# Tracing an attention's results one product later, behind that product's weights

## The chip, the cores and the metric

The kernel runs on one core of a Trainium2 chip. The metric is device microseconds from start to end of one execution; three runs of the kernel before gave a median of 849.12 us (848.67 to 849.75). TensorE (PE in the profile, its weight loads PEld) multiplies, VectorE (DVE) and ScalarE (ACT) compute elementwise, GpSimd (POOL) makes masks and starts some DMAs, SyncE (SP) starts the other DMAs. Each engine works through its own queue in order.

## The reference

One decoder layer: `x + W_out[conv, FoX, memory](RMSNorm(x))`, then an RMSNorm, for 512 tokens of 2048 features, all in float32.

```python
proj = rmsnorm(x, norm_g) @ w_in            # cut into the inputs of the three groups
u = silu(layernorm(causal_depthwise_conv(cv_a * sigmoid(cv_b), 31 taps)))
y_conv = (u @ w_conv_pw) * silu(cv_gate)
# FoX, 8 heads of 128: logit[t,s] = q.k * scale + c[t] - c[s], causal, c = cumsum(log_sigmoid(f))
y_fox = softmax(logit) @ v * silu(fox_gate)
# memory, 4 heads of 128: cross-attention into 256 memory tokens
y_mem = softmax(q.mk * scale) @ mv * silu(mem_gate)
out = rmsnorm(x + concat(y_conv, y_fox, y_mem) @ w_out, final_g)
```

## The kernel before

Every float32 operand is split into a high part (float32r, a copy on ScalarE, line 93) and a low part (the rest, a subtraction on VectorE, line 94). `split` makes both, and three matmuls (hh, hl, lh) stand for one. A piece of weights, 128x1024, is loaded by SP into one of six buffers `raw` and split into one of three buffers `wb` by `operand`, which remembers the low part's instruction in `lows`.

The projections of the layer are made two column blocks of 128 at a time in `pair`, from about 120 to 675 us: seven products of half the depth on sums of inputs and sums of weights (line 512) stand for eight. A product is 24 matmuls of 256 columns. In the order of `pair` they multiply `a11`, `s1`, `s2`, `a12`, `s4`, `s3` and `a22`; in the names of the trace `s1`, `s2` and `s3` are s0h, s1h and s2h (low parts s0l, s1l, s2l), the others hh and hl.

Beside each product, `beside` puts other work. One step of `bg`, mostly one of the 30 taps of the depthwise convolution (line 384, `acc` on VectorE), is queued on VectorE behind the product's split by `tc.issue_after(low)`: an edge of order for the instructions of that engine, not a wait. Then one piece of `slots` is traced, with its TensorE instructions behind the product's last matmul. A piece of an attention holds some matmuls into a buffer `at` (three of them, in PSUM) and what ScalarE and VectorE make of these at once. For a FoX head (counted from 0) the pieces are: scores and softmax of the query blocks 0 and 1 (`probs`: `mm3` into `at`, then line 899 adds the bias and takes the row's extreme on VectorE, line 903 is the exponential on ScalarE, lines 904 and 905 divide by the sum); the same for blocks 2 and 3; the gate and values (`gate_values`); transposes of the probabilities (`attend`, split into `pth` and `ptl`); the product with the values. The memory heads go the same way (`mem_probs`, `mem_attend`).

The order of instructions on an engine is not the order of tracing alone: a scheduler sorts what is traced by a timeline of its own, within the edges.

The convolution's layer norm (`norm`, `over_channels`) and its projection (`project_conv`, weights in `csh` and `csl`) come before head 7, and the output product (lines 1048 to 1142) last.

Of the kernel before, what the change touches and what calls it, by code (L numbers as in the profile page):

```python
# [14 lines left out]
ALU = mybir.AluOpType  # L15
AX = mybir.AxisListType

P = 128
# [29 lines left out]
def hybrid_layer_kernel(  # L48
# [18 lines left out]
    nc = tc.nc  # L67
    x, mem, out = x[0], mem[0], out[0]
# [11 lines left out]
    def nm(s):  # L80
        uid[0] += 1
        return f"{s}_{uid[0]}"
# [28 lines left out]

    bg, slots = deque(), deque()
    lows = [None]

    def background(n):
        for _ in range(min(n, len(bg))):
            bg.popleft()()

    def raw_tile(n, c):
        return wp.tile([P, n, c], F32, tag="raw", name=nm("raw"), bufs=6)
# [390 lines left out]

    def beside(low, mm):
        with tc.issue_after(low):
            background(1)
        if slots:
            with tc.issue_after(mm):
                slots.popleft()()
# [72 lines left out]
    def mem_probs(h, q, pr, i2):  # L592
        qh, ql = q
        sp = at((P, 2, M))
        for j in range(2):
            sl = slice((2 * i2 + j) * P, (2 * i2 + j + 1) * P)
            mm3(sp[:, j, :], (qh[:, sl], ql[:, sl]), (mk[0][:, h, :], mk[1][:, h, :]), True, True)
        ng = ma.tile([P, 2], F32, tag="ng", name=nm("ng"), bufs=4)
        nc.vector.tensor_reduce(ng, sp, AX.X, ALU.max, negate=True)
        nc.vector.tensor_scalar(ng, ng, SC, None, ALU.mult)  # L600
        pp = ma.tile([P, 2, M], F32, tag="pp", name=nm("pp"), bufs=2)
        sm = ma.tile([P, 2], F32, tag="sm", name=nm("sm"), bufs=4)
        for j in range(2):
            nc.scalar.activation(
                pp[:, j, :], sp[:, j, :], AF.Exp,
                bias=ng[:, j : j + 1], scale=SC, accum_out=sm[:, j : j + 1],
            )
        nc.vector.reciprocal(sm, sm)
        for j in range(2):
            nc.scalar.mul(pp[:, j, :], pp[:, j, :], sm[:, j : j + 1])  # L610
        pr.append(pp)

    def mem_attend(h, pr, gate):

        pts, ov = {}, []

        def transposes(mt):
            tp = at()
            for i in range(NT):
                nc.tensor.transpose(  # L620
                    tp[:, i * P : (i + 1) * P], pr[i // 2][:, i % 2, mt * P : (mt + 1) * P], ident
                )
            pts[mt] = tuple(ma.tile([P, S], F32R, tag=t, name=nm(t)) for t in ("th", "tl"))
            split(*pts[mt], tp)

        def values(mt):
            if mt == 0:
                ov.append(at())
            hs = slice(h * P, (h + 1) * P)
            mm3(ov[0], (mv[0][:, mt, hs], mv[1][:, mt, hs]), pts[mt], mt == 0, mt == MT - 1)  # L630

        def end():
            values(1)
            nc.vector.tensor_tensor(gate[0], ov[0], gate[0], ALU.mult)
            nc.gpsimd.dma_start(out=yd[12 + h], in_=gate[0])

        return [lambda: transposes(0), lambda: (values(0), transposes(1)), end]

# [2 lines left out]
    def after_mem(h):  # L641
        def f(xs, col):
            q = mem_query(xs)
            pr, gate = [], []
            pieces = mem_attend(*mpending.pop()) if mpending else [lambda: None]
            end = pieces.pop()
            pieces.append(
                lambda: (end(), gate.append(mem_gate(col)), mem_probs(h, q, pr, 0))
            )
            pieces.append(lambda: mem_probs(h, q, pr, 1))  # L650
            mpending.append((h, pr, gate))
            if h < NM - 1:
                (log_sigmoid, running_sum, forget_columns)[h]()
            else:
                pieces.extend(mem_attend(*mpending.pop()))
                after = pieces.pop()

                def close():
                    after()
                    mapool.close()  # L660
                    fgpool.close()
                    mpool.close()
                    open_fox()

                pieces.append(close)
            slots.extend(pieces)

        return f
# [109 lines left out]
    pieces = w_pieces()  # L778
# [80 lines left out]
    def gate_values(xs, col):  # L859
        fx = fox["pool"]  # L860
        gate = fx.tile([P, S], F32, tag="fgate", name=nm("fgate"), bufs=2)

        for x_, g in zip(xs, halves(gate)):
            nc.scalar.activation(g, x_, AF.Tanh, scale=0.5)
            nc.vector.scalar_tensor_tensor(g, g, 1.0, x_, ALU.add, ALU.mult)
        vp = at()
        for j in range(NT):
            sl = slice(j * P, (j + 1) * P)
            nc.tensor.transpose(vp[:, sl], col[:, sl], ident)
        v = tuple(fx.tile([P, NT, P], F32R, tag=t, name=nm(t)) for t in ("vh", "vl"))  # L870
        split(*v, vp.rearrange("p (j d) -> p j d", d=P))
        return gate, v

    def biases(h):
# [16 lines left out]
    def probs(q, k, i, b):  # L891
        fx = fox["pool"]
        n = (i + 1) * P
        sl = slice(i * P, n)
        w = max(n, M)
        sp = at((P, w))
        mm3(sp, (q[0][:, sl], q[1][:, sl]), (k[0][:, :w], k[1][:, :w]), True, True)
        ng = fx.tile([P, 1], F32, tag="ng", name=nm("ng"), bufs=4)
        nc.vector.tensor_tensor_reduce(
            b, sp[:, :n], b, 1.0, -MASKED, ALU.add, ALU.min, accum_out=ng  # L900
        )
        sm = fx.tile([P, 1], F32, tag="sm", name=nm("sm"), bufs=4)
        nc.scalar.activation(b, b, AF.Exp, bias=ng, scale=-1.0, accum_out=sm)  # L903
        nc.vector.reciprocal(sm, sm)
        nc.scalar.mul(b, b, sm)

    def attend(h, gv, pr):

        pth, ptl = fox["h"], fox["l"]

        def transposes(j):
            n = S - j * P
            tp = at((P, n))
            for i in range(j, NT):
                nc.tensor.transpose(
                    tp[:, (i - j) * P : (i - j + 1) * P], pr[i][:, j * P : (j + 1) * P], ident
                )
            w = max(n, M)
            split(pth[j][:, w - n :], ptl[j][:, w - n :], tp)

        def values():
            gate, (vh, vl) = gv
            ov = at()
            for j in range(NT):
                w = max(S - j * P, M)
                mm3(
                    ov[:, S - w :], (vh[:, j, :], vl[:, j, :]), (pth[j], ptl[j]),
                    j == 0, j == NT - 1,
                )
            if h < NH - 1:  # L930
                nc.vector.scalar_tensor_tensor(gate, ov, 0.5, gate, ALU.mult, ALU.mult)
                nc.gpsimd.dma_start(out=yd[4 + h], in_=gate)
            else:
                nc.vector.scalar_tensor_tensor(last["y"], ov, 0.5, gate, ALU.mult, ALU.mult)

        return [lambda: (transposes(0), transposes(1)), lambda: (transposes(2), transposes(3)), values]
# [12 lines left out]
    def after_gv(h):  # L949
        def f(xs, col):  # L950
            gv = []
            slots.append(lambda: gv.extend(gate_values(xs, col)))
            slots.extend(attend(h, gv, pr.pop(h)))
            if h == NH - 2:

                def norm():
                    fpool.close()
                    with tc.high_priority():
                        open_norm()
                        centre()  # L960
                        normalise()

                slots.append(norm)

        return f

# [19 lines left out]
    for fa, fb, then in work + [(None, None, None)]:  # L986
        if fa is not None:
            steps = pair(fa, fb)
            next(steps)
        else:  # L990
            for _ in range(2):
                load_piece()
            plain_ys()
            for _ in range(3):
                load_piece()
            heads = [load_y(4 + i // 2 + i % 2 * 4, i) for i in range(7)]
            last["y"] = y_room(7)
            for j in range(3):
                head_ys(j, *heads[2 * j : 2 * j + 2])
        if before:  # L1000
            before[1](*next(before[0]))
        if fa is None:
            while slots:
                slots.popleft()()
        else:
            next(steps)
            before = (steps, then)
            if fa == F_Q + (NH - 1) * P:
                project_conv()
                lnpool.close()  # L1010
                open_fox()
# [197 lines left out]
```

## Time and profile before

| | us |
|---|---|
| median of three runs | 849.12 |
| the profiled execution, its time | 849.81 |
| the profiled execution, its span | 848.0 |
| PE busy | 824.6 |
| DVE busy | 717.3 |
| ACT busy | 472.6 |

The span is the time from the first to the last instruction in the trace. Busy time of TensorE is modelled from pipelined matmuls, so the time that it loses is read better from the starts of matmuls that follow each other.

### The profile page before, as it was taken

How to read it: one execution, taken by the hardware profiler on the slowest of the kernel's cores; microseconds unless marked ns; L12 is line 12 of the kernel's file. 1: busy time of each engine (PE TensorE's matmuls, PEld its weight loads, DVE VectorE, ACT ScalarE, POOL GpSimd, SP SyncE). 2: the span in 40 equal slices, each digit the busy share in tenths (PEclk: the TensorE clock that was granted, in tenths of full speed). 3: DMA queues.
4: the chain of work that ended last, by engine and by line, in shares of the span. 5: the costliest groups of instructions: out<-in, count | busy, mean ns of one | idle time of the engine just before them, and what ended most of it. 6: DMA issues, size and time to landing. Idle time of an engine off the chain costs nothing. (4 is left out here: it accounts for less than half of the span.)

```text
span 848.0 us, 15403 instructions
## 1 busy us (share of the span) xinstructions
PE 824.6 (97%) x6212; PEld 785.7 (93%) x6212; DVE 717.3 (85%) x1047; ACT 472.6 (56%) x778; POOL 59.2 (7%) x86
## 2 busy tenths in 40 slices
PE   7999999999999999999999999999979999999996
PEld 6898889999999999999999999999979988998995
DVE  4589999999889998899988999896986976976964
ACT  4775457456775564554656455555564933442423
POOL 1012000000011000011110020200001000000001
PEclk8999999999999999999999999999989999999999
DMA  8983213434434342533434343445344627361515
GB/s 308 336 229 78 77 26 102 125 100 113 124 101 109 101 113 76 146 100 96 106 92 128 100 109 100 124 112 163 100 124 151 210 82 266 100 216 35 154 44 198
DMA packets 144262, 109.76 MB, mean 129 GB/s; under 512 B 4060, under 2 KB 127032, under 8 KB 143552
## 3 DMA queue, kind: packets, MB, share of 16 engines
q1 hardware_dynamic: 142272, 103.57, 42.5%
q0 software_dynamic: 1920, 5.23, 1.8%
q8 instruction: 48, 0.79, 0.4%
q14 instruction: 22, 0.18, 0.1%
HBM read 99.55 MB, written 9.22 MB: 128 GB/s over the span
## 5 line engine op out<-in xcount | busy, mean ns | idle before, releaser
L94 DVE TENSOR_TENSOR wb<-raw,wb 128x1024 fp32r<-128x1024 f32 x232 | 282.9, 1222 | 59.5 <-ACT wb L93 59.1
L93 ACT CAST wb<-raw 128x1024 fp32r<-128x1024 f32 x232 | 241.3, 1050 | 161.4 <-PE pj L550 49.7
L550 PE MATMUL pj<-hh,wb 128*128 128x256 f32 x1536 | 286.0, 281 | 0.5 <-ACT wb L93 0.4
L550 PEld LDWEIGHTS pj<-hh,wb 128*128 128x128 f32 x1536 | 240.7, 189 | 1.7 <-ACT wb L93 0.9
L550 PE MATMUL pj<-hl,wb 128*128 128x256 f32 x768 | 214.6, 279 | 0.0
L550 PEld LDWEIGHTS pj<-hl,wb 128*128 128x128 f32 x768 | 145.0, 189 | 0.8
L512 DVE TENSOR_TENSOR raw<-raw,raw 128x1024 f32<-128x1024 f32 x112 | 136.2, 1216 | 0.4
L384 DVE SCALAR_TENSOR_TENSOR acc<-up,cwt,acc 128x512 f32<-128x512 f32 x120 | 89.2, 743 | 0.0
L1110 PE MATMUL pj<-wb,rh 128*128 128x256 f32 x672 | 79.9, 279 | 0.7 <-DVE sst L1164 0.4
L1110 PEld LDWEIGHTS pj<-wb,rh 128*128 128x128 f32 x672 | 79.3, 188 | 1.4 <-DVE res L1036 1.1
L550 PE MATMUL pj<-s1h,wb 128*128 128x256 f32 x384 | 74.1, 284 | 3.8 <-DVE wb L94 3.8
L550 PE MATMUL pj<-s2h,wb 128*128 128x256 f32 x384 | 73.8, 280 | 0.0
L550 PE MATMUL pj<-s0h,wb 128*128 128x256 f32 x384 | 71.0, 278 | 0.0
L550 PEld LDWEIGHTS pj<-s1h,wb 128*128 128x128 f32 x384 | 60.1, 188 | 4.7 <-DVE wb L94 4.6
L550 PEld LDWEIGHTS pj<-s2h,wb 128*128 128x128 f32 x384 | 60.8, 188 | 0.1
L550 PEld LDWEIGHTS pj<-s0h,wb 128*128 128x128 f32 x384 | 60.2, 188 | 0.0
L550 PE MATMUL pj<-s2l,wb 128*128 128x256 f32 x192 | 53.6, 279 | 0.0
L550 PE MATMUL pj<-s0l,wb 128*128 128x256 f32 x192 | 53.5, 279 | 0.0
L550 PE MATMUL pj<-s1l,wb 128*128 128x256 f32 x192 | 53.4, 278 | 0.0
L884 POOL TENSOR_SCALAR_AFFINE_SELECT b<-b 128x128 f32<-128x128 f32 x32 | 29.8, 938 | 226.5 <-ACT b L883 226.4
L550 PEld LDWEIGHTS pj<-s2l,wb 128*128 128x128 f32 x192 | 36.1, 188 | 0.1
L550 PEld LDWEIGHTS pj<-s1l,wb 128*128 128x128 f32 x192 | 36.1, 188 | 0.0
(300 smaller groups left out, 1358.9 us busy)
## 6 DMA issues: line engine op xcount, KB each, us to landing
raw<-in_w_in_dram SPq DMA_DIRECT2D x104, 512.0 KB, 4.2
raw<-in_w_out_dram SPq DMA_DIRECT2D x32, 512.0 KB, 4.7
raw<-in_w_mem_kv_dram SPq DMA_DIRECT2D x12, 512.0 KB, 7.5
xr<-in_x_dram SPq DMA_DIRECT2D x4, 1024.0 KB, 7.9
res<-in_x_dram SPq DMA_DIRECT2D x8, 512.0 KB, 6.9
out_dram<-res SPq DMA_DIRECT2D x16, 256.0 KB, 2.9
rs<-yd SPq DMA_DIRECT2D x15, 256.0 KB, 4.4
mr<-in_mem_dram SPq DMA_DIRECT2D x8, 256.0 KB, 8.0
```

The lines of the kernel that those rows point to most:

```text
L93: ins = nc.scalar.copy(hi, src)
L94: low = nc.vector.tensor_tensor(lo, src, hi.bitcast(F32), ALU.subtract)
L384: return lambda: nc.vector.scalar_tensor_tensor(acc, up[:, j : j + S], cwt[:, c, j : j + 1], acc, ALU.mult, ALU.add)
L512: nc.vector.tensor_tensor(o, p, q, ALU.subtract)
L550: mm = nc.tensor.matmul(o, p[:, k, :], q, start=start and k == 0 and i == 0, stop=k == HK - 1 and i == 2, skip_group_check=True,)
L884: nc.gpsimd.affine_select(out=b[:, sl], in_=b[:, sl], pattern=[[-1, P]], compare_op=ALU.is_ge, fill=-MASKED, base=0, channel_multiplier=1,)
L1110: nc.tensor.matmul(o[:, m, :], p, q[:, k, :], start=start and k + m + i == 0, stop=k == HK - 1 and i == 2, skip_group_check=True,)
```

## The change

A new queue `after` takes what ScalarE and VectorE make of an attention's matmuls. It is emptied (`results`) in `beside` of the next product, inside `issue_after(low)`, so behind that product's weight split on VectorE, before the tap and before the next piece. `mem_probs` and `probs` hand over their softmax this way, the transposes and the values their splits, the value products their gating. Before a pair's results are handed on (`before[1]`) and in the last round the queue is emptied as well.

```diff
+    bg, slots, after = deque(), deque(), deque()
...
+    def results():
+        while after:
+            after.popleft()()
...
     def beside(low, mm):
         with tc.issue_after(low):
+            results()
             background(1)
         if slots:
             with tc.issue_after(mm):
...
             mm3(sp[:, j, :], (qh[:, sl], ql[:, sl]), (mk[0][:, h, :], mk[1][:, h, :]), True, True)
+        after.append(lambda: mem_softmax(sp, pr))
+
+    def mem_softmax(sp, pr):
...
-            split(*pts[mt], tp)
+            after.append(lambda: split(*pts[mt], tp))
...
-            nc.vector.tensor_tensor(gate[0], ov[0], gate[0], ALU.mult)
-            nc.gpsimd.dma_start(out=yd[12 + h], in_=gate[0])
+            after.append(gated)
...
-        split(*v, vp.rearrange("p (j d) -> p j d", d=P))
+        after.append(lambda: split(*v, vp.rearrange("p (j d) -> p j d", d=P)))
...
         mm3(sp, (q[0][:, sl], q[1][:, sl]), (k[0][:, :w], k[1][:, :w]), True, True)
+        after.append(lambda: softmax(sp, n, b))
+
+    def softmax(sp, n, b):
+        fx = fox["pool"]
         ng = fx.tile([P, 1], F32, tag="ng", name=nm("ng"), bufs=4)
...
-            split(pth[j][:, w - n :], ptl[j][:, w - n :], tp)
+            after.append(lambda: split(pth[j][:, w - n :], ptl[j][:, w - n :], tp))
...
+            after.append(lambda: gated(gate, ov))
...
-                slots.append(norm)
+                slots.append(lambda: after.append(norm))
...
         if before:
-            before[1](*next(before[0]))
+            columns = next(before[0])
+            results()
+            before[1](*columns)
         if fa is None:
             while slots:
+                results()
                 slots.popleft()()
+            results()
```

The scheduler's result differs from before in few places: on VectorE in the FoX heads 1, 2, 4 and 6, where 28 rows stand differently in all, and in one row of ScalarE. The rows of TensorE, SP and POOL are the same in kind and order. In the rows below, `ISA` with `b` and `ng` is line 899 (line 913 after), the read of a score tile `at`; `wb` is a piece of weights; `acc` is a tap (line 384, after 389).

VectorE in head 1, before, from the low part of the queries `fq` on (`wb_3378` is the third product's):

```order
L512 TENSOR_TENSOR raw_3226<-raw_3230,raw_3226 128x1024
L97 SCALAR_TENSOR_TENSOR fq_3294<-pj_2966,fq_3293 128x256
L899 ISA b_3305,ng_3359<-at_3355,b_3305 128x128
L899 ISA ng_3359 128x1
L94 TENSOR_TENSOR wb_3378<-raw_3226,wb_3378 128x1024
L384 SCALAR_TENSOR_TENSOR acc_2829<-up_2828,cwt,acc_2829 128x512
L899 ISA b_3310,ng_3369<-at_3365,b_3310 128x256
L899 ISA ng_3369 128x1
L94 TENSOR_TENSOR wb_3428<-raw_3232,wb_3428 128x1024
L384 SCALAR_TENSOR_TENSOR acc_2829<-up_2828,cwt,acc_2829 128x512
L94 TENSOR_TENSOR wb_3456<-raw_3230,wb_3456 128x1024
```

The first score read stands ahead of the third product's split. VectorE at the same place after (`wb_3366` is the third product's):

```order
L517 TENSOR_TENSOR raw_3226<-raw_3230,raw_3226 128x1024
L97 SCALAR_TENSOR_TENSOR fq_3294<-pj_2966,fq_3293 128x256
L94 TENSOR_TENSOR wb_3366<-raw_3226,wb_3366 128x1024
L913 ISA b_3305,ng_3393<-at_3355,b_3305 128x128
L913 ISA ng_3393 128x1
L389 SCALAR_TENSOR_TENSOR acc_2829<-up_2828,cwt,acc_2829 128x512
L913 ISA b_3310,ng_3399<-at_3359,b_3310 128x256
L913 ISA ng_3399 128x1
L94 TENSOR_TENSOR wb_3416<-raw_3232,wb_3416 128x1024
L94 TENSOR_TENSOR wb_3456<-raw_3230,wb_3456 128x1024
L389 SCALAR_TENSOR_TENSOR acc_2829<-up_2828,cwt,acc_2829 128x512
```

The split of the third product has moved ahead of the first score read, and the second tap behind the fifth product's split; the third tap comes only after the rows shown. Heads 2, 4 and 6 change here in the same way; heads 0, 3, 5 and 7 have the split ahead of the score read in both kernels.

TensorE in head 1, before, the scores of query blocks 2 and 3, with the engine whose event a row waits for:

```order
L104 MATMUL at_3406<-fk_3295,fq_3293 128x384 [waits PE_49]
L105 MATMUL at_3406<-fk_3296,fq_3293 128x384
L106 MATMUL at_3406<-fk_3295,fq_3294 128x384
L104 MATMUL at_3416<-fk_3295,fq_3293 128x512 [waits PE_49]
L105 MATMUL at_3416<-fk_3296,fq_3293 128x512
L106 MATMUL at_3416<-fk_3295,fq_3294 128x512
```

The same rows after:

```order
L104 MATMUL at_3406<-fk_3295,fq_3293 128x384 [waits PE_49]
L105 MATMUL at_3406<-fk_3296,fq_3293 128x384
L106 MATMUL at_3406<-fk_3295,fq_3294 128x384
L104 MATMUL at_3410<-fk_3295,fq_3293 128x512 [waits DVE_49]
L105 MATMUL at_3410<-fk_3296,fq_3293 128x512
L106 MATMUL at_3410<-fk_3295,fq_3294 128x512
```

The instructions stand as they did; the first matmul of the 512-column tile, the fourth score tile of the head, now waits for an event of VectorE where it waited for one of TensorE. This, in the same four heads, is the only wait of TensorE that differs.

## Rows read from the trace of the kernel before

**Rows 1.** The page, part 1: busy us (share of the span) and instructions by engine.
```profile
PE 824.6 (97%) x6212; PEld 785.7 (93%) x6212; DVE 717.3 (85%) x1047; ACT 472.6 (56%) x778; POOL 59.2 (7%) x86
```

**Rows 2.** Waits: engine and line, for whom; us in total, times, longest us.
```profile
DVE wb L94 <- ACT wb L93: 62.9, 69, 4.4
...
PE pj L104 <- ACT csh L93: 4.5, 1, 4.5
...
PE pj L550 <- DVE wb L94: 3.8, 4, 0.9
```

**Rows 3.** Stretches: us; PE, PEld, DVE, ACT, POOL busy (count); PEclk; DMA share; GB/s.
```profile
285.00:330.00 45.00, 44.06 (x371) 43.59 (x371) 42.68 (x63) 25.48 (x46) 2.82 (x5) 1.00 0.39 106
...
375.00:440.00 65.00, 65.00 (x550) 64.60 (x549) 60.48 (x88) 37.30 (x67) 11.62 (x10) 1.00 0.42 114
```

**Rows 4.** Timeline of PE, first place: start, us, engine, line, op, tiles, count [idle before].
```profile
284.95 0.28 PE L550 MATMUL pj<-s1h,wb 128*128 128x256 f32 x1
...
285.30 0.28 PE L550 MATMUL pj<-hl,wb 128*128 128x256 f32 x1
286.52 0.51 PE L550 MATMUL pj<-s1h,wb 128*128 128x256 f32 x2 [0.94 <-DVE wb L94]
286.86 0.28 PE L550 MATMUL pj<-s1l,wb 128*128 128x256 f32 x1
```

**Rows 5.** Timeline of PE, the second to fourth place.
```profile
330.91 0.28 PE L550 MATMUL pj<-hl,wb 128*128 128x256 f32 x1
332.13 0.50 PE L550 MATMUL pj<-s1h,wb 128*128 128x256 f32 x2 [0.94 <-DVE wb L94]
...
441.50 0.51 PE L550 MATMUL pj<-s1h,wb 128*128 128x256 f32 x2 [0.94 <-DVE wb L94]
...
550.88 0.51 PE L550 MATMUL pj<-s1h,wb 128*128 128x256 f32 x2 [0.94 <-DVE wb L94]
```

**Rows 6.** Timeline of DVE, first place.
```profile
285.03 0.29 DVE L899 CUSTOM_DVE_ANT_0 b<-at,b 128x128 f32<-128x128 f32 x1 [2.03 <-PE at L106]
285.24 1.22 DVE L94 TENSOR_TENSOR wb<-raw,wb 128x1024 fp32r<-128x1024 f32 x1
```

**Rows 7.** Timeline of ACT, the casts at the first three places.
```profile
282.75 2.00 ACT L93 CAST wb<-raw 128x1024 fp32r<-128x1024 f32 x2 [0.71 <-DVE raw L512]
...
284.91 1.05 ACT L93 CAST wb<-raw 128x1024 fp32r<-128x1024 f32 x1
...
328.24 2.00 ACT L93 CAST wb<-raw 128x1024 fp32r<-128x1024 f32 x2 [0.60 <-DVE raw L512]
...
436.92 1.99 ACT L93 CAST wb<-raw 128x1024 fp32r<-128x1024 f32 x2
```

**Rows 8.** Timelines of ACT, DVE and PE in head 3.
```profile
392.78 1.99 ACT L93 CAST wb<-raw 128x1024 fp32r<-128x1024 f32 x2
...
393.86 1.23 DVE L94 TENSOR_TENSOR wb<-raw,wb 128x1024 fp32r<-128x1024 f32 x1 [0.52 <-ACT wb L93]
...
396.04 0.39 PE L550 MATMUL pj<-s1h,wb 128*128 128x256 f32 x2
```

**Rows 9.** Timelines of DVE and PE near the first place.
```profile
313.42 1.31 DVE L94 TENSOR_TENSOR wb<-raw,wb 128x1024 fp32r<-128x1024 f32 x1
...
299.98 0.74 DVE L384 SCALAR_TENSOR_TENSOR acc<-up,cwt,acc 128x512 f32<-128x512 f32 x1
300.64 0.41 DVE L509 TENSOR_TENSOR col<-pj,p 128x256 f32<-128x256 f32 x1
...
301.52 0.28 PE L550 MATMUL pj<-hh,wb 128*128 128x256 f32 x1
...
289.72 0.39 PE L104 MATMUL at<-fk,fq 128*128 128x512 f32 x1
```

**Rows 10.** Timelines of DVE and PE around the convolution's norm.
```profile
619.17 0.69 DVE L717 TENSOR_SCALAR spare<-at 128x512 f32<-128x512 f32 x1 [0.55 <-PE at L686]
...
630.56 0.79 PE L104 MATMUL pj<-csh,wb 128*128 128x512 f32 x1 [4.48 <-ACT csh L93]
```

More of the change, by code (lines that the diff above doesn't have):

```diff
@@ L109, in queued @@
         tc.keep_in_program_order(nc.sync.dma_start(out=dst, in_=src))
-    bg, slots = deque(), deque()
+    bg, slots, after = deque(), deque(), deque()
     lows = [None]
@@ L630, in values, with gated @@
             mm3(ov[0], (mv[0][:, mt, hs], mv[1][:, mt, hs]), pts[mt], mt == 0, mt == MT - 1)
+        def gated():
+            nc.vector.tensor_tensor(gate[0], ov[0], gate[0], ALU.mult)
+            nc.gpsimd.dma_start(out=yd[12 + h], in_=gate[0])
         def end():
             values(1)
-            nc.vector.tensor_tensor(gate[0], ov[0], gate[0], ALU.mult)
-            nc.gpsimd.dma_start(out=yd[12 + h], in_=gate[0])
+            after.append(gated)
         return [lambda: transposes(0), lambda: (values(0), transposes(1)), end]
@@ L647, in f @@
             pieces.append(
-                lambda: (end(), gate.append(mem_gate(col)), mem_probs(h, q, pr, 0))
+                lambda: (end(), after.append(lambda: gate.append(mem_gate(col))), mem_probs(h, q, pr, 0))
             )
@@ L655, in f @@
                 pieces.extend(mem_attend(*mpending.pop()))
-                after = pieces.pop()
                 def close():
-                    after()
                     mapool.close()
@@ L663, in close @@
                     open_fox()
-                pieces.append(close)
+                pieces.append(lambda end=pieces.pop(): (end(), after.append(close)))
             slots.extend(pieces)
@@ L929, in values, with gated @@
                 )
+            after.append(lambda: gated(gate, ov))
+        def gated(gate, ov):
             if h < NH - 1:
```

## The prediction

> **What bounds the kernel now.** I read the page first: TensorE is busy 97% of the span [rows 1], so a microsecond counts only where TensorE loses it. Then TensorE's own waits: the longest is one of 4.5 us before the convolution's projection, the next, on VectorE's weight split, comes four times at 0.9 us [rows 2]. The table of stretches says how they lie: from 285 to 330 us TensorE is 0.94 us short of full, and from 375 to 440 it is full to the hundredth [rows 3]. So the four are single events, not a spread-out loss.
>
> The timeline of the first [rows 4]: matmuls of 256 columns start every 0.117 us (284.95 to 285.30 is three of them), and the next would have started at 285.42; it starts at 286.52. So 1.10 us are lost. Of the three that start from there to 286.86 the two intervals take 0.34 instead of 0.23 us, so starting up again costs another 0.11. The profile's 0.94 of idle time is less, since it counts from the modelled end of the last matmul. The other three places, at 332.13, 441.50 and 550.88, read alike [rows 5]: at the second the starts are 1.22 us apart again (330.91 to 332.13), and each has the same 0.94 of idle time.
>
> What TensorE waits for there is the low part of the third product's weights (its stationary operand is a piece of wb, the moving one is s2, which the trace calls s1h). VectorE at the first place [rows 6]: it is done with all else at 283.00, sits idle 2.03 us until TensorE has made the first score tile (L106), reads it (L899, 0.29 us) and only then makes the low part of wb, from 285.24, 1.22 us long. ScalarE had long finished the high part that this needs [rows 7]: two casts begin at 282.75 and take 2.00 together, one alone takes 1.05, so the first ends at 283.80. The weights were ready to be split 1.44 us before they were, behind an instruction that waited for TensorE. The four places have this in common, and they are the four heads in which the orders of the two kernels differ; the other four have the split in front of the score read already.
>
> **The change part by part.** No instruction is added or removed; TensorE's, SP's and POOL's rows stand in the same order. *Split ahead of the score read, four heads.* After the cast's end at 283.80 the split runs to about 285.05 (the row's 1.22, and 0.03 from cast to start, as the control below shows), and TensorE can go 0.06 later (286.46 to 286.52 in rows 4 and 6): 285.11. It is wanted at 285.42, or, if the weights are loaded one matmul's step ahead, at 285.30. That leaves 0.2 us. At the second place the cast begins at 328.24, so TensorE can go at 330.60, and wants to at 330.91: 0.3 us. At the third the cast begins at 436.92 [rows 7], so TensorE can go at 439.28 and wants to at 440.28 (1.22 before 441.50, where the first place has its 285.30): 1.0 us. The fourth is like the third. So all four waits go: 4 x (1.10 + 0.11) = 4.84 us.
>
> That this order runs without a wait the kernel itself shows in head 3 [rows 8]: VectorE waits 0.52 us for the cast that began at 392.78, starts the split at 393.86 (cast 1.05, then 0.03), and TensorE begins the matmul that needs it, at 396.04, with no idle time ahead of it.
>
> *What stands behind the split.* The score read waits for TensorE until 285.03 anyway; the split ends at 285.05, so the read loses 0.02 us, and ScalarE's exponential of this tile has to wait for a cast that ends only at 285.96 (284.91 and 1.05, rows 7). Behind the read everything on VectorE comes 1.2 us sooner, as TensorE does: the slack of later weights stays as it is. The bound from the other side is a split that runs as long as the longest row I saw, 1.31 instead of 1.22 [rows 9]: 0.09 of the 0.2 us.
>
> *Taps.* One or two of the 0.74 us convolution taps (L384) move behind later splits of the same head. From the first moved one on, the splits of that head stand 0.66 us sooner (a tap's step to the next start) or as before. The tightest later point is the column sum at 300.64, ending at 301.05, which the last product wants before 301.52 [rows 9]: in front of it there is now one tap fewer. Where the tap comes back, behind it, VectorE is as far as TensorE again. I take 0; the bounds are 0.66 us won and 0.66 us lost per head, 2.6 in all, if a split behind a tap had no room.
>
> *The fourth score tile.* There are three buffers for score tiles, so the 512-column scores reuse the buffer of the first, and TensorE now waits there for VectorE's read of it (before, an older TensorE event covered it). That matmul begins at 289.72 [rows 9], 1.2 sooner after the change, so 288.5; the read is done by 285.4. Cost 0, with 3 us of room.
>
> *ScalarE.* In one head a multiplication (L905) goes ahead of a cast that in that place waits for TensorE. ScalarE is busy 25.48 of 45 us [rows 3]. Cost 0.
>
> *Is the gain kept to the end?* The one big wait behind the four is 4.5 us at 630.56 for the convolution's norm [rows 2, 10]. If that chain ran on a time of its own, TensorE would only wait there longer. But it contains matmuls: VectorE's step at 619.17 was waiting for TensorE's sum (L686), so it comes forward with TensorE. Nothing later waits on a clock of its own; the loads are issued as buffers come free.
>
> The sum, against the profiled execution's 849.81: 849.81 - 4.84 = 844.97. The median shown is 849.12, 0.69 under that execution, so the prediction is 844.3.
>
> **The rivals.**
> 1. *The two tight places keep their wait.* For it: 0.2 and 0.3 us of room is what a slower cast or split could eat, and in the stretch from 285 to 330 VectorE is busy 42.68 of 45 us. Against it: VectorE's lead there grows by as much as TensorE's, and head 3 passes. If the first two waits stayed whole, 849.12 - 2 x 1.20 = 846.7.
> 2. *The gaps stay:* the ring of three score buffers, or of three wb, is what TensorE waits for, and VectorE only passes it on. For it: the four gaps are equal to a hundredth [rows 4, 5]. Against it: the cast into this wb was written by 283.80, so its buffer was there, and VectorE sat idle, waiting for a matmul [rows 6, 7]. 849.1. The Trainium skill (Perfetto Trace Analysis, section Optimization Strategy) has this as a rule: the same gap repeating on the engine that should be saturated can mean too little SBUF or PSUM for the next tile to be allocated. By that rule a new order on VectorE would win nothing; the trace disagrees, in the rows just named.
> 3. *The waits go but the end doesn't move:* the norm's 4.5 us grow by 4.8. For it: it is the longest wait [rows 2]; against it: rows 10. 849.1.
> 4. *Slower: VectorE is now held by the cast.* The split stands in front of the score read, the tap and the later splits, so a late cast holds them all. Before, the read went first. VectorE reaches the split at 283.00; up to a cast that ends at 284.00 nothing is lost, from 285.24 on the new order is worse than the old one by whatever it comes later. Elsewhere in the kernel the wait of a split for its cast is 0.9 us on average (62.9 in 69) and 4.4 at the longest [rows 2]. With the longest in all four heads the split would start at 287.40, 2.16 us later than before: 849.12 + 8.6 = 857.7. Against it: the cast begins 2.28 us before the score read at the first place (282.75 and 285.03), and there it is TensorE that both have to wait for.
> 5. *More is won,* the taps giving up to 0.66 us per head: 844.3 - 2.6 = 841.7. TensorE has no further wait in these heads that a tap could end, so hardly.
>
> **How the numbers follow.** My forecast 0.77, the tight places 0.09, the gaps staying 0.04, the norm 0.05, slower 0.04, more 0.01. A measurement of this kernel tells about 0.2% (1.7 us) from no change; by that the forecast, the tight places (2.4 us) and the last case are faster: 0.87, the same 0.09, slower 0.04. The forecast's own range is 843.2 to 845.6: the runs shown spread over 1.1 us, and up to half of the start-up cost may stay. To hold 8 in 10 the range goes to the tight places: 842.9 to 847.0.
>
> **What would show it.** In the profile of the changed kernel TensorE's wait for the split of wb in these products (3.8 us, four times) is gone, VectorE has the split in front of the score read in all heads, with a wait of under 1 us for the cast in its place, and the wait before the norm's products is still 4.5 us. Wrong would be: four waits of TensorE still there for L94 or for the score read, a wait of the norm grown to 9 us, or new waits on splits behind the moved taps.

## The result, and the profile after

The changed kernel takes 843.3 us (median of 4 runs, 842.85 to 844.69), against 849.43 for the kernel before beside it (4 runs, 848.67 to 850.31): a ratio of 0.993, with an interval of 0.9913 to 0.9947. The forecast was 844.3. The profiled execution took 842.94 us with a span of 841.1 (before: 849.81 and 848.0), so the two traces are 6.9 us apart and the medians 6.1; the forecast gain was 4.84. Lines of the file have moved: L550 is now L556, L899 is L913, L512 is L517, L384 is L389.

The engines' rows of the page, after (busy time, share of the span, instructions), show TensorE with 1.9 us less busy time than before in a span 6.9 us shorter [rows 1]:

```profile
PE 822.7 (98%) x6212; PEld 784.3 (93%) x6212; DVE 717.6 (85%) x1047; ACT 473.0 (56%) x778; POOL 62.0 (7%) x86
```

TensorE's own waits in the trace after (engine and line, for whom; us in total, times, longest):

```profile
PE pj L104 <- ACT csh L93: 4.5, 1, 4.5
PE pj L104 <- ACT mh L96: 2.7, 1, 2.7
PE at L198 <- POOL ident masks.py:199: 1.4, 1, 1.4
PE pj L1131 <- DVE sst L1185: 0.4, 1, 0.4
PE pj L556 <- ACT wb L93: 0.4, 1, 0.4
PE pj L1131 <- DVE res L1057: 0.3, 1, 0.3
```

The wait on VectorE's split, 3.8 us in four pieces [rows 2], is no longer in the list, no other has come in its place, and the norm's is 4.5 us as it was. The stretches from before the first place to behind the second, and around the third (us; PE, PEld, DVE, ACT, POOL busy and counts; PEclk; DMA share; GB/s), say the same: TensorE is full in both, where the first was 0.94 us short [rows 3].

```profile
284.10:329.10 45.00, 45.00 (x382) 44.73 (x381) 43.21 (x67) 26.93 (x48) 5.51 (x5) 1.00 0.40 106
372.80:437.60 64.80, 64.80 (x547) 64.40 (x547) 61.49 (x92) 37.61 (x68) 11.62 (x10) 1.00 0.43 114
```

The first place on TensorE, after:

```profile
284.07 0.28 PE L556 MATMUL pj<-s1h,wb 128*128 128x256 f32 x1
...
284.42 0.28 PE L556 MATMUL pj<-hl,wb 128*128 128x256 f32 x1
284.54 0.39 PE L556 MATMUL pj<-s1h,wb 128*128 128x256 f32 x2
284.77 0.28 PE L556 MATMUL pj<-s1l,wb 128*128 128x256 f32 x1
```

The row of 284.95 in [rows 4] now stands at 284.07, so 0.88 us were already won ahead of the first place, in the kernel's start. No instruction of the change lies there: the first row of VectorE that stands elsewhere is the split at 282.98 below. The pair that stood at 286.52 now follows its neighbour by 0.12 us, and the last row has gone from 286.86 to 284.77: 2.09 us earlier, of which 0.88 are the start and 1.21 are this place's, as the forecast had it (1.10 and 0.11).

VectorE at the first place, after, with the same columns:

```profile
282.98 1.23 DVE L94 TENSOR_TENSOR wb<-raw,wb 128x1024 fp32r<-128x1024 f32 x1 [0.84 <-ACT wb L93]
284.15 0.29 DVE L913 CUSTOM_DVE_ANT_0 b<-at,b 128x128 f32<-128x128 f32 x1
...
284.37 0.75 DVE L389 SCALAR_TENSOR_TENSOR acc<-up,cwt,acc 128x512 f32<-128x512 f32 x1
285.03 0.42 DVE L913 CUSTOM_DVE_ANT_0 b<-at,b 128x256 f32<-128x256 f32 x1
```

and ScalarE there:

```profile
281.89 2.00 ACT L93 CAST wb<-raw 128x1024 fp32r<-128x1024 f32 x2 [0.73 <-DVE raw L517]
...
284.05 1.05 ACT L93 CAST wb<-raw 128x1024 fp32r<-128x1024 f32 x1
285.00 0.40 ACT L917 ACTIVATE b<-b,ng 128x128 f32<-128x128 f32 x1
```

In place of 2.03 us idle for TensorE ahead of the score read [rows 6], VectorE waits 0.84 us for the cast and splits at once. The cast begins at 281.89, 1.05 us later it is 282.94, and the split starts at 282.98. With its 1.23 us the split is done at 284.21; 0.06 us behind that TensorE could go, at 284.27, and it goes at 284.54. So 0.27 us of room were left to the matmul, and 0.16 to its weight load, at 284.43; the prediction had 0.31 and 0.2. The read starts at 284.15 without a wait, and ScalarE's exponential (L917) follows the next cast at 285.00.

VectorE at the other three places, after, the split and the read behind it:

```profile
326.54 1.23 DVE L94 TENSOR_TENSOR wb<-raw,wb 128x1024 fp32r<-128x1024 f32 x1 [0.56 <-ACT wb L93]
328.52 0.29 DVE L913 CUSTOM_DVE_ANT_0 b<-at,b 128x128 f32<-128x128 f32 x1 [0.75 <-PE at L106]
...
434.64 1.23 DVE L94 TENSOR_TENSOR wb<-raw,wb 128x1024 fp32r<-128x1024 f32 x1 [0.52 <-ACT wb L93]
436.66 0.29 DVE L913 CUSTOM_DVE_ANT_0 b<-at,b 128x128 f32<-128x128 f32 x1 [0.79 <-PE at L106]
...
542.90 1.23 DVE L94 TENSOR_TENSOR wb<-raw,wb 128x1024 fp32r<-128x1024 f32 x1 [0.62 <-ACT wb L93]
544.81 0.29 DVE L913 CUSTOM_DVE_ANT_0 b<-at,b 128x128 f32<-128x128 f32 x1 [0.68 <-PE at L106]
```

VectorE still waits for TensorE there, but behind the split, where TensorE loses nothing by it. The wait of the split for its cast is 0.5 to 0.8 us, far from the 4.4 that the slower rival put in. That 4.4 was the wait of the kernel's first split, for weights that had yet to be loaded, and not one of the heads':

```profile
9.57 1.23 DVE L94 TENSOR_TENSOR wb<-raw,wb 128x1024 fp32r<-128x1024 f32 x1 [4.40 <-ACT wb L93]
```

The last piece of the gain is behind the norm. TensorE's rows there, after: the first product of the convolution's projection, and a later one with the low parts.

```profile
624.74 0.80 PE L104 MATMUL pj<-csh,wb 128*128 128x512 f32 x1 [4.48 <-ACT csh L93]
625.34 0.63 PE L104 MATMUL at<-csh,wb 128*128 128x512 f32 x1
625.76 0.63 PE L104 MATMUL pj<-csh,wb 128*128 128x512 f32 x1
...
629.29 0.40 PE L106 MATMUL pj<-csh,wb 128*128 128x512 f32 x1
```

The norm's wait is the same 4.48 us [rows 10] and comes 5.82 us sooner: 0.88 from the start and 4.94 for the four places, 1.24 each. The ends of the traces differ by 6.9, so another 1.1 us were won behind the wait. There the granted clock has fallen to its half, 1.2 GHz: matmuls of 512 columns start 0.42 us apart. The table of stretches from 0.5 us ahead of this matmul on, in the trace before and in the one after (the clock is the third number from the end):

```profile
630.06:638.06 8.00, 7.50 (x31) 6.73 (x32) 4.59 (x5) 2.40 (x5) 0.00 (x0) 0.64 0.00 1
```

```profile
624.24:632.24 8.00, 7.50 (x35) 6.55 (x36) 5.04 (x7) 3.01 (x5) 0.00 (x0) 0.79 0.00 0
```

A mean of 0.64 is 8 x 2 x 0.36 = 5.8 us at half speed, 0.79 is 3.4 us. Matmuls start 0.42 us apart in such time and 0.23 at full speed, so about half the work is done in it, and each microsecond less of it should be worth half a microsecond (below: the rule of halves): 2.4 us less are worth some 1.2 us, and 1.1 were found.

### The profile page after: what moved, and what is told of

It reads as the page before. It is cut to its first block, busy times and chain, and to the rows that moved or that the text cites. A ratio compares the mean times of both kernels' runs of the same rounds, so it can differ in the third digit from the quotient of the medians.

```text
span 841.1 us, 15403 instructions
## 1 busy us (share of the span) xinstructions
PE 822.7 (98%) x6212; PEld 784.3 (93%) x6212; DVE 717.6 (85%) x1047; ACT 473.0 (56%) x778; POOL 62.0 (7%) x86
## 5 line engine op out<-in xcount | busy, mean ns | idle before, releaser
L556 PE MATMUL pj<-hh,wb 128*128 128x256 f32 x1536 | 284.9, 280 | 0.5 <-ACT wb L93 0.4
L556 PEld LDWEIGHTS pj<-hh,wb 128*128 128x128 f32 x1536 | 239.8, 188 | 1.8 <-ACT wb L93 0.9
L556 PE MATMUL pj<-hl,wb 128*128 128x256 f32 x768 | 214.1, 279 | 0.0
L556 PEld LDWEIGHTS pj<-hl,wb 128*128 128x128 f32 x768 | 144.5, 188 | 0.8
L517 DVE TENSOR_TENSOR raw<-raw,raw 128x1024 f32<-128x1024 f32 x112 | 136.2, 1216 | 0.4
L389 DVE SCALAR_TENSOR_TENSOR acc<-up,cwt,acc 128x512 f32<-128x512 f32 x120 | 89.2, 743 | 0.0
L556 PE MATMUL pj<-s2h,wb 128*128 128x256 f32 x384 | 73.8, 280 | 0.0
L556 PE MATMUL pj<-s1h,wb 128*128 128x256 f32 x384 | 73.6, 283 | 0.0
L556 PE MATMUL pj<-s0h,wb 128*128 128x256 f32 x384 | 71.0, 278 | 0.0
L556 PEld LDWEIGHTS pj<-s2h,wb 128*128 128x128 f32 x384 | 60.7, 188 | 0.1
L556 PEld LDWEIGHTS pj<-s0h,wb 128*128 128x128 f32 x384 | 60.2, 188 | 0.0
L556 PEld LDWEIGHTS pj<-s1h,wb 128*128 128x128 f32 x384 | 60.1, 188 | 0.1
L556 PE MATMUL pj<-s2l,wb 128*128 128x256 f32 x192 | 53.6, 279 | 0.0
L556 PE MATMUL pj<-s0l,wb 128*128 128x256 f32 x192 | 53.5, 279 | 0.0
L556 PE MATMUL pj<-s1l,wb 128*128 128x256 f32 x192 | 53.3, 278 | 0.0
L894 POOL TENSOR_SCALAR_AFFINE_SELECT b<-b 128x128 f32<-128x128 f32 x32 | 32.6, 1025 | 219.6 <-ACT b L893 219.6
L556 PEld LDWEIGHTS pj<-s2l,wb 128*128 128x128 f32 x192 | 36.0, 188 | 0.1
L556 PEld LDWEIGHTS pj<-s1l,wb 128*128 128x128 f32 x192 | 36.1, 188 | 0.0
```

Source lines behind the costliest of these rows:

```text
L389: return lambda: nc.vector.scalar_tensor_tensor(acc, up[:, j : j + S], cwt[:, c, j : j + 1], acc, ALU.mult, ALU.add)
L517: nc.vector.tensor_tensor(o, p, q, ALU.subtract)
L556: mm = nc.tensor.matmul(o, p[:, k, :], q, start=start and k == 0 and i == 0, stop=k == HK - 1 and i == 2, skip_group_check=True,)
L894: nc.gpsimd.affine_select(out=b[:, sl], in_=b[:, sl], pattern=[[-1, P]], compare_op=ALU.is_ge, fill=-MASKED, base=0, channel_multiplier=1,)
```

## Experiments

**The theories.** The first, that of the prediction: the softmax's instructions on VectorE stood ahead of a split that was ready, in four heads, and putting them behind it returns 4.84 us; what the result has beyond that is the granted clock, behind the norm and in the start. The rival: the further deferrals of the change (the memory heads, the transposes, the values, the gates) or the moved taps bring the rest. The parts were separated first.

**The softmax alone.** Into the kernel before, only this goes in, with the queue that it needs:

```diff
         mm3(sp, (q[0][:, sl], q[1][:, sl]), (k[0][:, :w], k[1][:, :w]), True, True)
+        after.append(lambda: softmax(sp, n, b))
...
         with tc.issue_after(low):
+            results()
             background(1)
```

> The kernel before, with the FoX heads' softmax alone put off to behind the next product's split; the memory heads, the transposes, the values and the gating stay as they were before. My theory is that the four score reads on VectorE are all that counts: as fast as the full change, 6.1 us (5 to 7) under the kernel before, with no wait of TensorE for the split of wb in the pairs. The rival, that the other results put off (splits of the transposes, gating, memory softmax) give a part of the gain: less than 4.8 us, by 1 us or more.

Measured: 843.21 us (843.06 to 844.55, 5 runs), against 849.88 for the kernel before on the same chip: 0.9926 (0.9913 to 0.9938). The whole gain is in this part. In its trace the wait for the split is gone, as in that of the changed kernel, and every engine's instructions stand in the same order as there. So the scheduler makes the same queues of both, and the gains of 6.1 and 6.7 us are two measurements of one order.

**All of the change but the softmax.**

```diff
-        after.append(lambda: softmax(sp, n, b))
+        softmax(sp, n, b)
```

> The changed kernel, with the FoX heads' softmax traced at once again and everything else still put off. My theory: the four waits of TensorE for the split (3.8 us in the profile, 0.94 each) are back, and the time is that of the kernel before within 1 us. The rival, that the other parts give a share: 1 us or more under it.

Measured: 849.89 us (848.67 to 851.33, 11 runs), a ratio of 1.0003 (0.9994 to 1.0011). TensorE's waits in its trace:

```profile
PE pj L104 <- ACT csh L93: 4.5, 1, 4.5
PE pj L556 <- DVE wb L94: 3.8, 4, 0.9
```

The four waits are back with their size, and the time is that of before. All instructions stand in the order of the kernel before, so the other deferrals move nothing on any engine; that they bring nothing and cost nothing holds for what this scheduler makes of them.

**The softmax deferred in heads 0 to 2 only.** Then the first two places change, the tight ones, and the other two don't.

```diff
-        after.append(lambda: softmax(sp, n, b))
+        if later:
+            after.append(lambda: softmax(sp, n, b))
+        else:
+            softmax(sp, n, b)
...
+                slots.append(lambda i=i: [probs(q, k, j, pr[h][j], h < 3) for j in (i, i + 1)])
```

> The changed kernel, with the softmax put off in the FoX heads 0, 1 and 2 alone; in heads 4 and 6 the score read stands ahead of the split again. If each of the four places costs 1.21 us by itself: two waits of 0.94 us are left, at heads 4 and 6, and the time lies 2.4 us above that of the FoX softmax alone (all four). If the waits pass their loss on (a gain at the first place eaten by the next, or one late place making the later ones late): less than 1 us or more than 4 us above it, and the idle time of each of the two is not 0.94 us.

Measured: 846.93 us (846.13 to 847.86, 5 runs), 0.9965 (0.9952 to 0.9979): 2.95 us under the kernel before and 3.7 over the softmax alone, in the medians. TensorE at the two places that were left:

```profile
439.04 0.51 PE L556 MATMUL pj<-s1h,wb 128*128 128x256 f32 x2 [0.94 <-DVE wb L94]
...
548.43 0.50 PE L556 MATMUL pj<-s1h,wb 128*128 128x256 f32 x2 [0.94 <-DVE wb L94]
```

In the trace before they are at 441.50 and 550.88 [rows 5]; they come 2.46 and 2.45 us earlier, twice 1.23. So the price of a place adds up, and the two tight places give theirs whole. The 3.7 in place of 2.4 are not explained by the places: this trace has a longer time at half speed behind the norm than that of the softmax alone, and the start of before, which comes 0.9 us later (last section). Its stretch behind the norm:

```profile
627.58:635.58 8.00, 7.50 (x32) 6.68 (x33) 4.62 (x6) 2.83 (x5) 0.00 (x0) 0.70 0.00 1
```

0.70 is 4.8 us at half speed, 1.0 less than before, worth 0.5 us by the rule of halves. Its end is 2.8 us earlier than before's (spans 845.2 and 848.0), and 2.46 + 0.5 is 3.0.

**The clock.** To see what the clock adds, the norm's wait was filled: 24 matmuls of the next projection are issued ahead of the convolution's projection, while ScalarE and VectorE make the norm.

```diff
             if fa == F_Q + (NH - 1) * P:
+                before = (iter([next(steps)]), then)
+                results()
                 project_conv()
```

> The changed kernel, with the last product of head 7's query and key pair traced ahead of the convolution's projection instead of behind it, so that TensorE has 24 matmuls (2.8 us) more in front of the 4.5 us wait for csh. If the chain of the norm doesn't grow: the wait falls to about 1.7 us and the time by 2.8 us against the full change, a little more if the granted clock then no longer falls to 0.5 for 3.4 to 6.8 us behind the wait. The rival: the product's weights have to be differenced (1.21 us) and split (1.22 us) on VectorE, which is busy with that same chain; then csh comes 1.2 to 2.4 us later and the time falls by 0.4 to 1.6 us only.

Measured: 840.44 us (839.61 to 841.09, 4 runs), 0.989 (0.9876 to 0.9903): 2.8 us under the softmax alone, and faster than both kernels. TensorE around the norm in its trace:

```profile
622.53 0.36 PE L556 MATMUL pj<-hh,wb 128*128 128x256 f32 x1 [1.73 <-DVE col L514]
...
625.40 0.40 PE L104 MATMUL pj<-csh,wb 128*128 128x512 f32 x1
625.63 0.40 PE L104 MATMUL at<-csh,wb 128*128 128x512 f32 x1
625.87 0.39 PE L104 MATMUL pj<-csh,wb 128*128 128x512 f32 x1
```

and its stretch:

```profile
624.90:632.90 8.00, 7.92 (x41) 6.41 (x40) 6.95 (x8) 5.24 (x8) 0.00 (x0) 1.00 0.23 66
```

The wait is now 1.73 us in front of the added matmuls, the projection begins without one, the clock is 1.00, and the matmuls that started 0.42 us apart start 0.23 apart. The gain in the medians is about what the wait alone gives (4.48 - 1.73 = 2.75). By the rule of halves the clock should have returned another 1.4 us on top, half of the 2.9 us of matmuls that the trace after has at half speed, and it isn't in the result. In the traces 0.9 us of it are there at first: from the last matmul ahead of the wait to the first of the product on s1 that follows the projection (s0h) it is 22.76 us after (619.99 to 642.75) and 19.13 with the wait filled (620.52 to 639.65), 3.63 less, of which the wait is 2.75. To the last matmul of the kernel it is only 2.5 less. A part of the loss is seen: at full speed TensorE waits for the low parts that VectorE makes (csl). The weight load's row:

```profile
626.58 0.19 PEld L105 LDWEIGHTS pj<-csl,wb 128*128 128x128 f32 x1 [0.52 <-DVE csl L94]
```

Two more such waits of the weight load, 0.37 us for a cast and 0.49 for a split, stand at the products on rs that follow, at 655.94 and 657.41. The rest stays open.

**The filled kernel with and without the deferred softmax.** With the wait filled, no stretch at half speed lies behind the norm, so this pair weighs the change without that share of the clock. The kernel without it has again the line `softmax(sp, n, b)` in place of the deferral; the other is the filled kernel unchanged.

> The filled kernel (last product of head 7's pair ahead of the convolution's projection) with the FoX softmax traced at once again, so with the four score reads ahead of the split. In the traces so far each of the four places costs 1.24 us, 4.94 in all, but the medians of the change lie 6.1 to 6.7 us under the kernel before. If the difference of 1.2 to 1.8 us comes from the granted clock behind the norm's wait (0.5 for 6.8 us in the kernel before, for 3.4 in the changed one), then without that wait it is gone: the time lies 4.9 us (4.4 to 5.4) above the filled kernel with the change, and the clock is 1.00 from 600 to 700 us in both. If it comes from the four places, more lost there than one trace shows: 6.1 to 6.7 us above.

> The filled kernel with the change once more, on the same chip as the run without it. Both theories: 9.4 us under the kernel before, as in its first run (840.4 against 849.9), within 0.8 us; the wait of TensorE ahead of the norm's products 1.7 us instead of 4.5, clock 1.00 there.

Measured, on one chip: 845.25 us (844.9 to 846.2, 5 runs) without and 840.72 (839.46 to 841.31, 4 runs) with the deferral; against the kernel before, 848.91 there, 0.9952 (0.9939 to 0.9966) and 0.9896 (0.9883 to 0.991). TensorE's waits without it:

```profile
PE pj L556 <- DVE wb L94: 3.8, 4, 0.9
...
PE pj L556 <- DVE col L514: 1.7, 1, 1.7
```

with the stretches from 600 to 700 us, first without it, then with it:

```profile
600.00:700.00 100.00, 98.15 (x640) 88.53 (x639) 83.25 (x139) 63.30 (x110) 3.30 (x8) 1.00 0.48 152
```

```profile
600.00:700.00 100.00, 98.14 (x622) 87.71 (x622) 82.92 (x138) 63.11 (x109) 3.30 (x8) 1.00 0.49 160
```

The clock is 1.00 in both, and the difference is 4.5 us in the medians (4.8 against the filled kernel's first runs, on another chip) and 4.9 in the spans (844.5 and 839.6; a start 0.47 us later in the second, and as much won back behind 600 us, cancel there). Where no half-speed stretch lies behind the norm, the change is worth its four places within about half a microsecond. The 6.1 and 6.7 us of the unfilled kernels then hold over 1 us that isn't the places'. By its interval the 6.1 may be 4.5 to 7.4, so that pair alone doesn't show this; the softmax run's 6.7 (5.3 to 7.4) and the rows of the traces do.

One expectation was missed: the filled kernel is 8.2 us under the kernel before on this chip, not 9.4 within 0.8. It repeats to 0.3 us (840.44 and 840.72); it is the kernel before whose median is 1.0 us lower here (848.91, against 849.88).

Not tried: a fourth buffer of weights, which would have put the second rival to the test in its own way. The softmax run decides that rival anyway: the buffers are the same there, and the gaps are gone.

## Why the prediction was right, and where its size was off

- *The four stalls.* Right in place and in size: 4.84 us forecast, 4.94 between the traces by the norm, 4.5 to 4.9 in the filled pair.
- *The room at the places.* 0.16 us to the weight load at the first (0.2 forecast). At the second the cast begins at 325.46 in the trace after; the start and the first place have moved all there by 0.88 + 1.24 = 2.12 us, so in the old time that is 327.58, not the forecast 328.24: the room was about 1.0 us rather than 0.3. The 0.66 us between them is VectorE's lead: the sum of weights (L517) that the cast waited for comes 2.80 us sooner (324.15, before 326.95), where TensorE has moved by 2.12. About 0.5 us of the lead come from the moved tap. It now stands behind an earlier such sum, and the next split waits 0.29 us for its cast, where it waited 0.79; three splits that took 0.1 us less than before give most of the rest. So the taps, taken at 0, did give VectorE something, but into room, not into time. The split before and after, and the cast after:

```profile
306.24 1.23 DVE L94 TENSOR_TENSOR wb<-raw,wb 128x1024 fp32r<-128x1024 f32 x1 [0.79 <-ACT wb L93]
```

```profile
303.73 1.23 DVE L94 TENSOR_TENSOR wb<-raw,wb 128x1024 fp32r<-128x1024 f32 x1 [0.29 <-ACT wb L93]
...
325.46 2.00 ACT L93 CAST wb<-raw 128x1024 fp32r<-128x1024 f32 x2
```

- *The score read.* 0.02 us of loss forecast; it starts without a wait.
- *Taps, fourth score tile, ScalarE.* All at 0, and no wait of TensorE for any of them is in the list after.
- *The norm.* It moved along with its 4.48 us, as said; the third rival is out. What the prediction left out was the clock behind that wait. It treated the end as moving along rigidly, but the time at half speed there was 2.4 us shorter, and this gave 1.1 us more in the traces. That is the missing term behind the change; the start gave 0.9 more. With 4.94 for the places they make the 6.9 us between the traces, where the sum had 4.84. The medians differ by 6.1, and how much of the 1.3 over the sum is the one or the other they don't tell.
- *The rivals.* The tight places went with the others (heads 0 to 2); the buffers were not the cause (softmax alone). The Trainium skill (Perfetto Trace Analysis, section Optimization Strategy) says that a repeating gap can mean too little SBUF or PSUM; here it meant something else: the gap came from in-order queueing on VectorE, and a new order ended it. The slower case took the longest wait of a split for its cast, 4.4 us, which belongs to the kernel's first weights; 0.5 to 0.8 were found. The taps gave no time.

What is not settled: why the time at half speed behind the norm was shorter after the change. Whether the change has a part in it, or the two traces differ by chance, one trace of each kernel can't show. The 0.88 us of the start are not the change's: no instruction differs there, and the starts of the traces lie up to 1.8 us apart (last section).

## What to carry to other kernels

When the bound engine waits for a helper engine, look at what the helper did before that instruction: if it sat idle in an in-order queue, behind an instruction that waits for the bound engine itself, a change of order on the helper is worth the whole wait and the restart, as it was here, and the places add up. The room is read from the producer's time (here the cast's end), not from the wait. Where a long wait stays behind the change, leave a microsecond of the range for the clock behind it.

## What the runs showed of the hardware

Behind the same wait of 4.48 us, with the same instructions, the granted clock's time at half speed differed from trace to trace. The first matmul behind the wait, a later one of the projection (L105), the time between the two, and the mean clock in the 7.5 us from the first on:

| trace | first | later one | between | clock |
|---|---|---|---|---|
| before | 630.56 | 638.04 | 7.48 | 0.65 |
| after | 624.74 | 631.14 | 6.40 | 0.81 |
| softmax alone | 624.73 | 631.37 | 6.64 | 0.78 |
| all but the softmax | 631.44 | 639.31 | 7.87 | 0.59 |
| heads 0 to 2 | 628.08 | 635.13 | 7.05 | 0.71 |

The rule of halves holds in all of them: the clocks stand for 5.3, 2.9, 3.3, 6.2 and 4.4 us at half speed, and with half of that taken off, 4.8 to 5.0 us are left each time. So a kernel's end can be a microsecond sooner or later though the instructions around the wait stand the same. It also differs from run to run of one kernel: of the eleven runs of all but the softmax, the four with a mean clock of 0.990 have spans of 848.4 to 849.5 us, the seven with 0.991 to 0.994 spans of 846.6 to 847.8. What decides between the lengths was not found.

The start differs in the same way. The first projection, which waits for the first weights (ScalarE casts them and then makes mh), and a matmul some 6 us later, before, after and with the softmax alone:

```profile
9.97 1.22 PE L104 MATMUL pj<-wb,mh 128*128 128x512 f32 x2 [3.39 <-ACT mh L96]
...
16.34 0.40 PE L106 MATMUL pj<-wb,ml 128*128 128x512 f32 x1
```

```profile
9.47 0.97 PE L104 MATMUL pj<-wb,mh 128*128 128x512 f32 x2 [2.74 <-ACT mh L96]
...
15.44 0.39 PE L106 MATMUL pj<-wb,ml 128*128 128x512 f32 x1
```

```profile
9.06 1.22 PE L104 MATMUL pj<-wb,mh 128*128 128x512 f32 x2 [1.52 <-ACT mh L96]
...
12.68 0.63 PE L105 MATMUL pj<-wb,mh 128*128 128x512 f32 x1
13.10 0.63 PE L104 MATMUL pj<-wb,mh 128*128 128x512 f32 x1
...
15.44 0.39 PE L106 MATMUL pj<-wb,ml 128*128 128x512 f32 x1
```

Both later traces lead by 0.90 us at the second row, and not for the same reason. After, 0.50 us come from the weights (their cast begins at 8.00 in place of 8.50) and 0.40 from the matmuls between the rows, with 1.1 us less at half speed: the mean clock over the 6.37 us from the first row on is 0.73 after and 0.64 before. With the softmax alone the weights give it all, 0.91 (the cast begins at 7.59), and the time from row to row is that of before. The profile's clock for this start reads 1.00, but the matmuls of 512 columns start 0.42 us apart up to 13.5 us, as at half speed: this trace holds no record of the clock ahead of 13.7 us. So it is worth reading the clock off the starts of the matmuls as well. With all but the softmax the start is 0.9 us behind that of before (the row of 284.95 stands at 285.85), so 1.8 us lie between the starts of two traces.
